# Queries of the sparse attention projected with features on the partitions, split once ahead of it, and loaded as matmul operands by DMA

## The chip, the cores and the metric

The kernel runs on one core of one Trainium2 chip. A core has five engines that run their own instruction streams in order: TensorE (PE in the profile, its weight loads PEld), VectorE (DVE), ScalarE (ACT), GpSimd (POOL) and SyncE (SP, which mostly issues DMAs). They share an on-chip memory of 128 partitions, and PE writes its products into accumulator banks of 128 partitions by 512 fp32, of which the kernel uses eight. The metric is the device time of one execution in microseconds (us), lower is better. On one core an execution is one program of 30086 recorded instructions.

## The reference

The reference is one decoder layer over 1024 positions and 1024 channels, in float32: an RMS norm and one input projection, three mixers side by side (a Mamba-2 scan, stick-breaking attention, and a sparse attention with three branches), a gated merge, an output projection, and a gated MLP with a short convolution. What matters here is the sparse attention and where its queries come from:

```python
h = rms_norm(x, pre_mix_norm[l])
proj = h @ w_in[l]                       # 512 of its columns are nsa_q: 2 groups x 4 heads x 64 features
...
sc = einsum('bqghd,bngd->bghqn', qb, kc) * scale - slopes * dist_c      # 64 compressed keys per group
p_cmp = masked_softmax(sc, dist_c >= 0)
o_cmp = einsum('bghqn,bngd->bqghd', p_cmp, vc)
... p_cmp summed over the 4 heads ranks 16 blocks of 64 keys; the best 8 are kept ...
ss = einsum('bqghd,bgqnkd->bghqnk', qb, ks) * scale - slopes * dist_s   # selected blocks
sw = einsum('bqghd,bkgd->bghqk', qb, kwb) * scale - slopes * dist_w     # window of 512
out = gate0 * o_cmp + gate1 * o_sel + gate2 * o_win
```

The query is used three times: against the compressed keys, against the selected blocks and against the window.

## The kernel before

**Products in three parts.** A float32 value is kept as a pair of rounded halves, `hi` and `lo` (type fp32r), and a product a*b is summed from a_hi*b_hi, a_hi*b_lo and a_lo*b_hi. So whatever enters such a product is first split: ScalarE copies it to fp32r (`hi`), and VectorE or GpSimd subtracts (`lo`). All of PE's instructions go through one helper, so they carry line 234; the tile names tell them apart (`ps_s`, `ps_t`, `ps_o`, `ps_b` and `dense` are accumulator banks; there are two each of `ps_s`, `ps_t` and `dense`, one each of `ps_o` and `ps_b`).

**The program's stages, in order.** (1) The start, to about 56 us: x comes in twice, by rows (for the norm's sums of squares, `square`) and by columns, and the query projection runs while the norm's factors are still being formed. `h_hi` and `h_lo` hold the columns, 8 chunks `k` of 128 channels by 1024 positions, in two halves `h` of 512 positions. The first half is first split without the norm's factor (`first_split`), so that its queries are scaled afterwards, and then normed and split again (`norm`, `high`, `low`). (2) A gate unit, and the Mamba projections (`ssm_units`), to about 310 us. (3) The sparse attention (`nsa_stage`): projections of keys and values, the compressed keys and values (two units, `unit_steps(U_CMP + s)`), the keys turned onto the partitions, then the loop over 16 tiles, from 395 to about 725 us. (4) Stick-breaking attention, the scan, the merge and the MLP, which the change does not touch.

**Queries, up to now.** `four_tiles` (L497) computes for a chunk `ci` (one of the two key groups, 256 query features) and a half `h` four tiles of 128 positions. In `tm_products` (L424) the positions are the stationary operand and the 256 features of the weights move through the array, so a result has positions on the partitions; each of the two chunks and two halves takes 8 k by 4 tiles by 3 matmuls of 256 columns. `q_out` (L528) scales a tile, for the first half by the norm's factor of its positions (`rq`, a value per partition), and `q_store` (L534) writes it to memory as `q_d[group, tile]`. The order of this stage is pinned by hand on every engine (`pin`), with two hooks at given places of the second group of products: `first_rows` and `second_rows` let PE transpose the norm's factors into a row per half (`rows`), which VectorE multiplies into x.

**The loop of the sparse attention.** Three generators are advanced in slots: `compressed` (L1024), which runs ahead and makes a tile's compressed branch, its ranking and its query operands; `maxima` (L1109), which bounds the scores; and `attend` (L1148), which makes scores and values, block by block. PE's order is the order of this program (`E.in_order[0] = True`). A slot in which there is no block takes matmuls of the gate units as filling (`fill.take`, `NSA_FILL`), two groups of three; a slot with a block takes one group where `compressed` and `maxima` have nothing to do. `NSA_SLOTS`, `NSA_START` and the lags set the slots. On the other engines and on SP's queue a scheduler places instructions.

**What a tile does with its query.** `compressed` loads the tile as it lies in memory (`q_in`, L1026), and a second time with every head twice side by side (`qd`, two DMAs, L1029). PE transposes `q_in` in two pieces, ScalarE copies them to `qT` (L1034), and PE multiplies `qT` with the compressed keys `KC`. Four lags and the softmax later PE transposes `qd` in four pieces into `p1`; ScalarE rounds all 128 rows to `Q2` (L1093) and the upper 64 to `Q1` (L1094), and VectorE leaves `Q2`'s lower half as the rest (L1099). `Q1` holds the hi part with mask rows and slopes below it, from a ring of 4 tiles; the two slope rows come by a DMA on ScalarE's queue (L1096) once per ring tile and group. `score` (L1152) multiplies `Q1` and `Q2` with the keys.

## Time and profile before

| | us |
|---|---|
| three runs, median (lowest to highest) | 2168.35 (2167.76 to 2170.72) |
| the profiled execution: its own time | 2170.24 |
| the profiled execution: span of the instructions | 2168.5 |
| PE busy in the span | 2110.4 (97%) |
| VectorE, ScalarE, GpSimd busy | 1349.0, 1209.9, 1188.1 (62%, 56%, 55%) |
| DMA, mean rate over the span | 108 GB/s |

The span is that of the profiled execution, whose own time is 1.7 us longer. In the profile's rows a start and a duration are given in us from the span's start. A matmul's duration reaches from its entry into the array to its modelled end, while the next one has already entered; what a matmul takes of PE's time is the distance from its start to the next one's start. "x4" in a row joins four instructions; an fp32 matmul that is not fp32r stands as two. In brackets stands the idle time before an instruction and what ended it. In the table by windows the columns are each engine's busy time with its count, then PE's granted clock (1.00 is full), the DMA engines' busy share and the rate.

### The profile page before, as it was taken

The page shows a single profiled execution, that of the slowest core. Times are in us where ns is not written, and L with a number is a line of the kernel's source. Part 1 is how long each engine was busy: PE and PEld are TensorE (multiplying, and loading weights), DVE is VectorE, ACT ScalarE, POOL GpSimd, SP SyncE. Part 2 cuts the span into 40 slices and gives each one's busy share as a digit, 9 for nine tenths or more (in the row PEclk, how much of TensorE's full clock was granted, in tenths as well). Part 3 has the DMA queues.
Part 4 walks back from the last instruction along what each step waited for, and adds up shares of the span by engine and source line. Part 5 has one row for each costly group of instructions (what it writes and reads, how often), then busy time and mean ns, then how long its engine had stood idle before and what let it go on. Part 6 is the DMA issues. An engine that isn't in the chain of part 4 may idle for free.

```text
span 2168.5 us, 30086 instructions
## 1 busy us (share of the span) xinstructions
PE 2110.4 (97%) x10437; PEld 1712.7 (79%) x10437; DVE 1349.0 (62%) x2665; ACT 1209.9 (56%) x2290; POOL 1188.1 (55%) x1035
## 2 busy tenths in 40 slices
PE   9999999999999999999999999999999999999997
PEld 9787888876676688888877778887778888888886
DVE  7865545247667416566547876238776677686776
ACT  6544442367867746677775553236554454476634
POOL 0276742136846834334326686557777777766733
PEclk9999999999999999999999999999999999999999
DMA  7223341321221011222344522435222223265432
GB/s 268 96 101 112 112 138 54 92 92 42 62 71 38 23 63 40 69 68 97 119 172 169 176 93 93 146 100 187 88 83 90 96 100 114 97 198 178 149 119 105
DMA packets 127457, 233.48 MB, mean 108 GB/s; under 512 B 29844, under 2 KB 43828, under 8 KB 127304
## 3 DMA queue, kind: packets, MB, share of 16 engines
q1 hardware_dynamic: 124584, 228.94, 32.0%
q10 hardware_dynamic: 2720, 2.62, 0.4%
q8 instruction: 82, 1.34, 0.3%
q14 instruction: 71, 0.58, 0.1%
HBM read 170.06 MB, written 61.45 MB: 107 GB/s over the span
## 4 chain that ended last, share of the span: by engine, by line
PE 66%; DVE 7%; ACT 3%; issue 2%; POOL 2%; DMA 1%; SPq 0%; DVEq 0%; ACTq 0%; POOLq 0%
PE dense L234 46%; PE ps_s L234 7%; PE ps_o L234 5%; PE ps_t L234 3%; PE psn L234 3%; PE ps_b L234 2%; POOL wlo L307 1%; ACT wT L1159 1%; DVE u L344 0%; DVE ps_t L1127 0%; DMA lo<-m_d 0%; DVE x L1855 0%; DVE x L2053 0%; ACT ps_b L1049 0%; ACT oT L1183 0%
## 5 line engine op out<-in xcount | busy, mean ns | idle before, releaser
L307 POOL TENSOR_TENSOR wlo<-wraw,whi 128x256 fp32r<-128x256 f32 x300 | 237.4, 823 | 236.2 <-ACT whi L302 232.5
L234 PE MATMUL dense<-h_hi,whi 128*128 128x512 f32 x656 | 262.2, 400 | 1.1 <-DVE kk L913 1.1
L234 PE MATMUL dense<-h_hi,wlo 128*128 128x512 f32 x656 | 257.6, 393 | 0.0
L234 PE MATMUL dense<-h_lo,whi 128*128 128x512 f32 x656 | 257.1, 392 | 0.0
L1170 POOL TENSOR_TENSOR wT_lo<-wT,wT_hi 128x512 fp32r<-128x512 f32 x132 | 168.2, 1289 | 66.4 <-ACT wT_hi L1169 54.6
L234 PE MATMUL dense<-x,uhi 128*128 128x512 f32 x600 | 191.4, 391 | 0.8 <-ACT x L751 0.8
L234 PE MATMUL dense<-hi,wlo 128*128 128x512 f32 x448 | 176.4, 395 | 0.3 <-POOL wlo L668 0.3
L234 PE MATMUL dense<-lo,whi 128*128 128x512 f32 x448 | 174.8, 391 | 1.1 <-POOL lo L1874 1.1
L234 PE MATMUL dense<-hi,whi 128*128 128x512 f32 x448 | 174.8, 390 | 0.0
L668 POOL TENSOR_TENSOR wlo<-wraw,whi 128x1024 fp32r<-128x1024 f32 x35 | 84.6, 2419 | 110.0 <-ACT whi L667 109.8
L234 PEld LDWEIGHTS dense<-h_hi,wlo 128*128 128x128 f32 x656 | 123.6, 188 | 27.0
L234 PEld LDWEIGHTS dense<-h_hi,whi 128*128 128x128 f32 x656 | 123.9, 189 | 24.1 <-issue 1.3
L677 POOL TENSOR_TENSOR ulo<-uf,uhi 128x1024 fp32r<-128x1024 f32 x35 | 84.2, 2405 | 106.5 <-ACT uhi L676 106.4
L234 PEld LDWEIGHTS dense<-h_lo,whi 128*128 128x128 f32 x656 | 124.0, 189 | 23.0
L302 ACT ACTIVATE whi<-wraw 128x1024 fp32r<-128x1024 f32 x76 | 80.4, 1057 | 108.4 <-PE dense L234 91.9
L234 PEld LDWEIGHTS dense<-x,uhi 128*128 128x128 f32 x600 | 112.5, 188 | 25.9 <-ACT x L751 1.7
L1393 POOL TENSOR_TENSOR s_lo<-sa,s_hi 128x512 fp32r<-128x512 f32 (+2 forms) x48 | 54.2, 1130 | 129.3 <-ACT s_hi L1392 129.3
L344 DVE SCALAR_TENSOR_TENSOR u<-dense,pv,u 128x510 f32<-128x510 f32 (+1 forms) x140 | 103.5, 742 | 34.5 <-ACT u L340 34.0
L680 POOL TENSOR_TENSOR ulo<-uf,uhi 128x1024 fp32r<-128x1024 f32 x35 | 84.1, 2402 | 41.1 <-ACT uhi L679 35.1
L234 PE MATMUL dense<-x,ulo 128*128 128x512 f32 x264 | 103.2, 391 | 0.0
L1159 ACT ACTIVATE wT<-ps_s 128x512 f32<-128x512 f32 x132 | 78.2, 595 | 39.6 <-PE ps_s L234 33.2
L234 PEld LDWEIGHTS dense<-hi,wlo 128*128 128x128 f32 x448 | 84.1, 188 | 20.3 <-issue 1.9
(591 smaller groups left out, 6132.1 us busy)
## 6 DMA issues: line engine op xcount, KB each, us to landing
wraw<-in_wfm SPq DMA_DIRECT2D x62, 512.0 KB, 3.7
wraw<-in_wup SPq DMA_DIRECT2D x48, 512.0 KB, 3.5
lo<-m_d SPq DMA_DIRECT2D x58, 256.0 KB, 3.7
g_d<-gate_e SPq DMA_DIRECT2D x48, 256.0 KB, 2.2
s_d<-o SPq DMA_DIRECT2D x48, 256.0 KB, 2.1
m_d<-u SPq DMA_DIRECT2D x44, 256.0 KB, 2.0
row<-g_d SPq DMA_DIRECT2D x36, 256.0 KB, 4.0
row<-s_d SPq DMA_DIRECT2D x32, 256.0 KB, 5.4
```

The costliest lines, as they stand in the source:

```text
L234: return pin(f(*a, **k), in_order)
L302: act(hi, raw, AF.Copy)
L307: eng.tensor_tensor(lo[:, s], raw[:, s], fl(hi[:, s]), op=OP.subtract)
L344: V.scalar_tensor_tensor(o[:, d:], ps[:, :512 - d], taps[d], o[:, d:], op0=OP.mult, op1=OP.add)
L668: eng.tensor_tensor(wlo, raws[0], fl(whi), op=OP.subtract)
L677: eng.tensor_tensor(l24, f24, fl(h24), op=OP.subtract)
L680: eng.tensor_tensor(l31, f31, fl(h31), op=OP.subtract)
L1159: act(w.rearrange("p h q -> p (h q)"), pz, AF.Exp)
L1170: P.tensor_tensor(lo, wf, fl(hi), op=OP.subtract)
L1393: (P if SB_SLO else V).tensor_tensor(s_lo[:, c0:], a[:, c0:], fl(s_hi[:, c0:]), op=OP.subtract)
```

## The change

The queries are projected the other way round: the weights are the stationary operand and 512 positions move, so a result has 128 features on the partitions and a half of the positions along them. `q_units` replaces `four_tiles`: per chunk and half 2 units by 8 k by 3 matmuls of 512 columns. All eight results are scaled by 1/8 on ScalarE as they leave; the first half's norm factor is now a row along the positions, so VectorE copies the transposed row of the first half to on-chip memory (`row0`) and GpSimd multiplies four results of 128x512 with it ahead of their store. `q_d` becomes a table of 512 features by 1024 positions. The hooks move from (3, 0) and (7, 0) of four tiles per k to (4, 0) and (7, 1) of two units per k.

At the start of the sparse attention the whole table is read back in eight pieces of 128x512, split by ScalarE and GpSimd, and written out as two tables, `qh_d` and `ql_d`: eight loads and sixteen stores on SP's queue. A tile of the loop then loads `qT` from `q_d` and the operands from these tables: the hi part to `Q1`'s upper half and to `Q2`'s upper half, the lo part to `Q2`'s lower half, 64 features by 4 heads by 128 positions in each DMA, runs of 512 bytes. The six transposes of a tile, the copies L1034, L1093 and L1094 and the subtraction L1099 are gone. The slope rows are loaded by SP. The ring of `Q1` and that of `Q2` have 5 tiles instead of 4, that of `qT` 3 instead of 1. `compressed` has one step fewer in all, with five waiting steps (`CMP_LAG`) instead of four ahead of the transposes of the softmax.

```diff
 
 T_AT = 3
+Q_ROWS = 4
+CMP_LAG = 5
 
...
 
 
-    q_d = scratch("q_d", [2, 8, 128, 256])
+    q_d = scratch("q_d", [512, T])
 
...
             pin(V.scalar_tensor_tensor(h_lo[:, k, hs(0)], x, pre[:, k:k + 1], fl(hi), op0=OP.mult, op1=OP.subtract))
 
-    def four_tiles(ci, ws, h, banks, hooks={}):
+    def q_units(ci, ws, h, banks, hooks={}):
 
         pss = [f() for f in banks]
         for k in range(8):
+            hi, lo = ws[k // 2]
             for n, ps in enumerate(pss):
                 if (k, n) in hooks:
                     hooks[k, n]()
-                tm_products(ps, ci, ws, 4 * h + n, k)
+                s = slice((k % 2) * 256 + n * 128, (k % 2) * 256 + (n + 1) * 128)
+                for m, (a, b) in enumerate(((hi, h_hi), (lo, h_hi), (hi, h_lo))):
+                    mm(ps, a[:, s], b[:, k, hs(h)], start=k == 0 and m == 0, stop=k == 7 and m == 2)
         return pss
...
     def factor(h, between=()):
 
-        rt, rq, v = [n1p.tile([128, 4], F32, name=f"r{n}", bufs=2) for n in "tqv"]
+        rt, v = [n1p.tile([128, 4], F32, name=f"r{n}", bufs=2) for n in "tv"]
         rsqrt_mean(rt, v, stats[h], DM)
...
         rb = n1p.tile([128, 4, 128], F32, name="rb")
         pin(act(rb, rt[:, :, None].to_broadcast([128, 4, 128]), AF.Copy))
-        if h == 0:
-            pin(V.tensor_scalar(rq, rt, 0.125, None, op0=OP.mult))
-        return rq, rb
+        return rb
 
...
         return r
 
-    def q_out(q, n, ps, scale, eng=None):
-        if eng is V:
-            pin(V.tensor_scalar(q[:, n], ps[:, :256], scale, None, op0=OP.mult))
-        else:
-            pin(act(q[:, n], ps[:, :256], AF.Copy, scale=scale))
+    def q_out(q, n, ps):
+        pin(act(q[:, n], ps, AF.Copy, scale=0.125))
 
     def q_store(ci, h, q):
-        pin(nc.scalar.dma_start(q_d[ci, 4 * h:4 * h + 4].rearrange("t p c -> p t c"), q))
+        pin(nc.scalar.dma_start(q_d[ci * 256:(ci + 1) * 256, hs(h)].rearrange("(n p) t -> p n t", p=128), q))
 
     def q_tile(name):
-        return wx0.tile([128, DM], F32, name=name).rearrange("p (t c) -> p t c", t=4)
+        return wx0.tile([128, DM], F32, name=name).rearrange("p (n t) -> p n t", n=2)
 
...
         for t in (6, 7):
             square(t)
-        late.append(factor(1)[1])
+        late.append(factor(1))
         norm(0, 4)
+        row0 = ev.tile([128, 512], F32, name="o")
+        pin(V.tensor_copy(row0, rows[0]))
+        rows.append(row0)
 
     def second_rows():
-        rows.append(factor_rows(late[0], ps_s))
+        rows.insert(1, factor_rows(late[0], ps_s))
 
...
     for p in range(2):
         chunk_weights(1, p)
-    pss = four_tiles(0, tm0, 0, (ps_s, ps_s, ps_t, ps_t))
+    first = q_units(0, tm0, 0, (ps_t, ps_t))
     for t in range(4):
         square(t)
-    rq, rb = factor(0, [partial(chunk_weights, 1, 2)])
-    qs = [q_tile("ulo")]
-    for n, ps in enumerate(pss):
-        q_out(qs[0], n, ps, rq[:, n:n + 1], V)
+    rb = factor(0, [partial(chunk_weights, 1, 2)])
     for t in (4, 5):
         square(t)
-    pss = four_tiles(1, tm1, 0, (ps_o, ps_d, ps_d, ps_b), {(3, 0): first_rows, (7, 0): second_rows})
-    qs.append(q_tile("uhi"))
+    second = q_units(1, tm1, 0, (ps_d, ps_d), {(Q_ROWS, 0): first_rows, (7, 1): second_rows})
+    qs = [q_tile("ulo"), q_tile("uhi")]
+    for n, ps in enumerate(first):
+        q_out(qs[0], n, ps)
     for k in range(8):
...
         if k > 1:
             low(1, k - 2)
-        for n in ((0, 3), (1,), (2,))[k] if k < 3 else ():
-            q_out(qs[1], n, pss[n], rq[:, n:n + 1])
         if k > 2:
             high(0, k - 3)
+    for n, ps in enumerate(second):
+        q_out(qs[1], n, ps)
     for h in range(2):
+        for n in range(2):
+            pin(P.tensor_tensor(qs[h][:, n], qs[h][:, n], rows[2], op=OP.mult))
         q_store(h, 0, qs[h])
...
     for k in range(8):
         low(0, k)
-    pss = four_tiles(0, tm0, 1, (ps_t, ps_t, ps_o, ps_b))
+    pss = q_units(0, tm0, 1, (ps_o, ps_b))
     qs.append(q_tile("ulo"))
     for n, ps in enumerate(pss):
-        q_out(qs[2], n, ps, 0.125)
+        q_out(qs[2], n, ps)
     q_store(0, 1, qs[2])
     all_in_order[0] = False
-    pss = four_tiles(1, tm1, 1, (ps_d, ps_s, ps_s, ps_t))
+    pss = q_units(1, tm1, 1, (ps_t, ps_t))
     qs.append(q_tile("uhi"))
     for n, ps in enumerate(pss):
-        q_out(qs[3], n, ps, 0.125)
+        q_out(qs[3], n, ps)
     q_store(1, 1, qs[3])
...
     nc.sync.dma_start(pos.rearrange("p s b l q -> p (s b l q)"), A["pos"])
     half = [slice(0, 64), slice(64, 128)]
+    qh_d, ql_d = [E.dram.tile([512, T], F32, name=n, tag=n) for n in ("qh_d", "ql_d")]
+    for g, h, n in itertools.product(range(2), range(2), range(2)):
+        r, c = slice((2 * g + n) * 128, (2 * g + n + 1) * 128), E.hs(h)
+        x, hi, lo = [ck.tile([128, 512], dt, name=f"q{m}", bufs=2) for m, dt in zip("xhl", (F32, R32, R32))]
+        nc.sync.dma_start(x, q_d[r, c])
+        act(hi, x, AF.Copy)
+        P.tensor_tensor(lo, x, fl(hi), op=OP.subtract)
+        nc.sync.dma_start(qh_d[r, c], fl(hi))
+        nc.sync.dma_start(ql_d[r, c], fl(lo))
     for s in range(2):
...
     for x in MMs + augs:
         V.memset(x, 0.0)
-    Q1s = [wk.tile([128, 512], R32, name=f"Q1_{n}", bufs=1) for n in range(4)]
+    Q1s = [wk.tile([128, 512], R32, name=f"Q1_{n}", bufs=1) for n in range(5)]
     for x in Q1s:
...
 
     def compressed(g, i):
-        qs = wk.tile([128, 256], F32, name="q_in", bufs=3)
-        nc.sync.dma_start(qs, q_d[g, i])
-        qd = wk.tile([128, 4, 2, 64], F32, name="qd", bufs=2)
-        for n in range(2):
-            nc.sync.dma_start(qd[:, :, n, :], q_d[g, i].rearrange("p (h d) -> p h d", h=4))
-        pq = ps_b()
-        for a in range(2):
-            tr(pq[:, a * 128:(a + 1) * 128], qs[:, a * 128:(a + 1) * 128], ident)
-        qT = wk.tile([128, 2, 128], F32, name="qT", bufs=1)
-        act(qT.rearrange("p a b -> p (a b)"), pq[:, :256], AF.Copy)
-        yield
-        ps = pq[:, 256:]
+        qT = wk.tile([128, 2, 128], F32, name="qT", bufs=3)
+        ts = slice(i * 128, (i + 1) * 128)
+        nc.sync.dma_start(qT, q_d[g * 256:(g + 1) * 256, ts].rearrange("(a p) t -> p a t", p=128))
+        Q1 = Q1s[(8 * g + i) % 5]
+        Q2 = wk.tile([128, 512], R32, name="Q2", bufs=5)
+        hi, lo = [x[g * 256:(g + 1) * 256, ts].rearrange("(h d) t -> d h t", d=64) for x in (qh_d, ql_d)]
+        for dst, x in ((Q1[0:64], hi), (Q2[0:64], hi), (Q2[64:128], lo)):
+            nc.sync.dma_start(fl(dst).rearrange("p (h t) -> p h t", h=4), x)
+        if i < 5:
+            nc.sync.dma_start(fl(Q1[80:82, :]), qa_d[:, g, :])
+        if g and i < 4:
+            act(Q1[64:80, :], fl(Q1[64:80, :]), AF.Copy, scale=0.0)
+        ps = ps_b()[:, :256]
         for a in range(2):
...
             V.tensor_tensor(left, left, im, op=OP.is_equal)
             V.tensor_scalar(aug[:, 64:80], left, NEG, None, op0=OP.mult)
-        for _ in range(4):
+        for _ in range(CMP_LAG):
             yield
...
         yield
 
-        Q1 = Q1s[i % 4]
-        Q2 = wk.tile([128, 512], R32, name="Q2", bufs=4)
-        p1 = ps_b()
-        for h in range(4):
-            tr(p1[:, h * 128:(h + 1) * 128], qd[:, h].rearrange("p a d -> p (a d)"), ident)
-        act(Q2, p1, AF.Copy)
-        act(Q1[0:64, :], p1[0:64], AF.Copy)
-        if i < 4:
-            nc.scalar.dma_start(fl(Q1[80:82, :]), qa_d[:, g, :])
-            if g:
-                act(Q1[64:80, :], fl(Q1[64:80, :]), AF.Copy, scale=0.0)
-        V.tensor_tensor(Q2[64:128, :], p1[64:128], fl(Q2[64:128, :]), op=OP.subtract)
-        yield
         yield
```

**Where instructions move.** PE at the start of the loop of tiles: `thi` and `h_lo` are the last value projection's operands, `q_in` the query as loaded, `KC` the compressed keys, `dense` a gate unit. Before:

```order
L234 MATMUL ps_s<-thi,h_lo 128x296
L234 MATMUL ps_b<-ident,q_in 128x128 x2
L234 MATMUL dense<-h_hi,whi 128x512
L234 MATMUL dense<-h_lo,whi 128x512
L234 MATMUL dense<-h_hi,wlo 128x512
L234 MATMUL dense<-h_hi,whi 128x512
L234 MATMUL dense<-h_lo,whi 128x512
L234 MATMUL dense<-h_hi,wlo 128x512
L234 MATMUL ps_b<-KC_2783,qT 128x128 x2
```

and with the change:

```order
L236 MATMUL ps_s<-thi,h_lo 128x296
L236 MATMUL ps_b<-KC_2578,qT 128x128 x2
L236 MATMUL dense<-h_hi,whi 128x512
L236 MATMUL dense<-h_lo,whi 128x512
L236 MATMUL dense<-h_hi,wlo 128x512
L236 MATMUL dense<-h_hi,whi 128x512
```

The product with the compressed keys now stands directly behind the projections, and all of the ten groups of gate matmuls up to the softmax's transposes (`cp`) stand behind it; before two of the ten stood ahead of it.

ScalarE at the same place (`da` belongs to the scan's decays, the third row is the slope rows' DMA). Before:

```order
L278 ACTIVATE sg<-sg 128x192
L1004 ACTIVATE da<-da 128x128
L1096 DMA Q_0_3673<-qa_d 2x512
L1034 ACTIVATE qT<-ps_b 128x256
L1096 DMA Q_1_3674<-qa_d 2x512
L1096 DMA Q_2_3675<-qa_d 2x512
L1096 DMA Q_3_3676<-qa_d 2x512
L1049 ACTIVATE ps_b,m_3713<-ps_b,m_3713 128x64 x4
```

and with the change:

```order
L280 ACTIVATE sg<-sg 128x192
L1017 ACTIVATE da<-da 128x128
L1063 ACTIVATE ps_b,m_3558<-ps_b,m_3558 128x64 x4
L278 ACTIVATE gate_e<-dense 128x512
L279 ACTIVATE gate_e<-gate_e 128x512
```

The slope rows' DMAs and the copy to `qT` have left ScalarE; the exponentials of the first softmax are next. VectorE keeps its order there: the clearing of the `Q1` ring (L1022, now L1035 and five times instead of four) stands ahead of the addition of the bias to the first scores.

SP's queue with the change, from the last key store to the second tile:

```order
L987 DMA k_d_2921<-k_3225 128x1024
L1040 DMA qT<-q_d 128x2x128
L1045 DMA Q_0_3534<-qh_d 64x4x128
L1045 DMA Q_3546<-qh_d 64x4x128
L1045 DMA Q_3546<-ql_d 64x4x128
L1047 DMA Q_0_3534<-qa_d 2x512
L1054 DMA cbias<-in_c_bias 128x256
L1040 DMA qT<-q_d 128x2x128
```

Where a tile had four DMAs (`q_in`, `qd` twice, `cbias`), it has five, and a sixth in the first five tiles of a group.

## The prediction

> **What bounds the kernel now.** I read the page first, for the busy shares and the chain that ended last.
>
> ```profile
> PE 2110.4 (97%) x10437; PEld 1712.7 (79%) x10437; DVE 1349.0 (62%) x2665; ACT 1209.9 (56%) x2290; POOL 1188.1 (55%) x1035
> PE 66%; DVE 7%; ACT 3%; issue 2%; POOL 2%; DMA 1%; SPq 0%; DVEq 0%; ACTq 0%; POOLq 0%
> ```
>
> PE is busy 97% of the span and carries two thirds of the chain, so a matmul taken away is worth its distance to the next one, unless PE waits there anyway. That differs by stage, so I read the table by windows next: a stretch of dense 512-column matmuls, and the sparse attention's loop with its beginning and its densest part.
>
> ```profile
> 100.00:125.00 25.00, 25.00 (x110) 20.33 (x109) 10.23 (x15) 11.71 (x18) 15.59 (x10) 1.00 0.32 105
> 395.40:410.00 14.60, 10.93 (x42) 8.69 (x41) 6.09 (x19) 5.68 (x19) 0.00 (x0) 0.77 0.10 29
> 410.00:722.00 312.00, 296.83 (x1517) 220.64 (x1516) 195.14 (x657) 220.38 (x502) 185.94 (x212) 1.00 0.21 62
> 550.00:600.00 50.00, 48.11 (x248) 32.94 (x247) 29.78 (x92) 44.01 (x100) 41.22 (x40) 1.00 0.23 62
> ```
>
> A 512-column matmul costs 25 / 110 = 0.227 us. From 410 to 722 us PE is busy 296.83 of 312 us, 95%: the loop is PE's, though ScalarE comes near (44.01 of 50 us from 550 on). Its beginning is another matter: PE works 10.93 of 14.60 us, at a mean granted clock of 0.77.
>
> **The loop.** Each of 16 tiles loses two transposes of `q_in` and four of `qd`. Their durations (0.27 us each) overlap; what they cost is read from starts in PE's timeline, one group of each kind with its neighbours.
>
> ```profile
> 414.13 0.60 PE L234 MATMUL ps_b<-ident,qd 128*128 128x128 f32 x4
> 414.48 0.48 PE L234 MATMUL dense<-h_hi,whi 128*128 128x512 f32 x1
> 414.80 0.39 PE L234 MATMUL dense<-h_lo,whi 128*128 128x512 f32 x1
> 415.03 0.40 PE L234 MATMUL dense<-h_hi,wlo 128*128 128x512 f32 x1
> 594.85 0.38 PE L234 MATMUL ps_b<-ident,q_in 128*128 128x128 f32 x2
> 594.99 0.47 PE L234 MATMUL ps_o<-wT_hi,V_hi 128*65 128x512 f32 x1
> 595.29 0.39 PE L234 MATMUL ps_o<-wT_hi,V_lo 128*65 128x512 f32 x1
> ```
>
> Four transposes hold PE 0.35 us, and the matmul behind them takes 0.32 to the next start where its like takes 0.23: 0.44 in all. Two hold it 0.14, and the one behind them takes 0.30 instead of 0.23: 0.21. A tile loses 0.65 us, 16 tiles 10.4 us. The other engines lose work too, by the views of the tiles `Q` and `qT`, and a wait goes, by the groups of PE:
>
> ```profile
> L1093 ACT ACTIVATE Q<-ps_b x16: 577/593/605, 415.6 to 711.7; 128x512 fp32r<-128x512 f32 x16
> L1094 ACT ACTIVATE Q<-ps_b x16: 577/584/592, 416.1 to 712.2; 64x512 fp32r<-64x512 f32 x16
> L1034 ACT ACTIVATE qT<-ps_b x16: 375/383/392, 400.4 to 696.3; 128x256 f32<-128x256 f32 x16
> L234 PE MATMUL ps_b<-ident,q_in 128*128 128x128 f32 x32 | 6.3, 280 | 1.0 <-DVE Q L1105 1.0
> ```
>
> ScalarE loses 0.593 + 0.584 + 0.383 = 1.56 us a tile, 25 us in all. With the transposes goes their wait of 1.0 us for the single bank `ps_b`. Bounds: if PE's waits in the loop grow to take half of what is freed, 5.2 us stay; if ScalarE's relief also counts where it is nearly full, 1.56 - 0.65 = 0.9 us in each of the six tiles without gate filling add 5.4, and the loop gains 10.4 + 1.0 + 5.4 = 16.8. I take 9.5: the 10.4 and the 1.0, less 1.9 because matmuls that covered other engines' latencies are gone; PE's 95% speaks for the near side.
>
> What replaces the transposes comes by DMA in shapes that no row shows. The nearest, issue and landing:
>
> ```profile
> L1029 SPq DMA_DIRECT2D qd<-q_d x32: 529/546/1135, 386.5 to 672.2; - x32
> DMA to landing us min/median/max: 2.5/2.7/3.4
> ```
>
> `qd` lands in runs of 256 bytes, the new loads in runs of 512; I take 3.4 us, the slow end. Four issues of 0.55 and a landing of 3.4 make 5.6 us. They are issued at `compressed`'s first step; `maxima` wants `Q1` nine steps later, most of a tile, and a tile takes 312 / 16 = 20 us. The ring of five is free in time: tile k's loads write where tile k-5 stood, and `compressed` runs at most three tiles ahead. SP issues one DMA more a tile, 0.55 us in 20. So the loads are hidden, at nothing; wholly uncovered they would cost 16 x 5.6 = 90 us, which is why they have a rival below.
>
> **The loop's beginning,** rows of PE, VectorE and ScalarE in order of time, and the table's stretch of low clock:
>
> ```profile
> 395.43 0.38 PE L234 MATMUL ps_b<-ident,q_in 128*128 128x128 f32 x2
> 399.18 2.51 DVE L1022 TENSOR_TENSOR Q<-edges 64x512 fp32r<-64x512 f32 x4
> 399.90 0.49 ACTq L1096 DMA_DIRECT2D Q<-qa_d  x1
> 400.44 0.38 ACT L1034 ACTIVATE qT<-ps_b 128x256 f32<-128x256 f32 x1 [2.29 <-DVE Q L1022]
> 400.88 1.22 PE L234 MATMUL ps_b<-KC,qT 128*128 128x128 f32 x4 [3.67 <-ACT qT L1034]
> 402.19 0.43 DVE L1044 TENSOR_TENSOR ps_b<-ps_b,cbias 128x256 f32<-128x256 f32 x1 [0.51 <-issue]
> 405.62 0.35 DVE L1053 TENSOR_SCALAR cp<-cp,some 128x256 f32<-128x256 f32 x1
> 409.34 0.38 PE L234 MATMUL ps_b<-ident,cp 128*128 128x128 f32 x2
> 399.30:406.10 6.80, 5.22 (x14) 4.32 (x15) 4.20 (x9) 2.00 (x9) 0.00 (x0) 0.50 0.21 61
> ```
>
> The copy to `qT` stands in ScalarE's queue behind the slope rows' DMA, and that waits for VectorE to clear the first `Q1`; PE waits 3.67 us for it. The change takes both off ScalarE, so PE does the `KC` product at 395.4, when the last projection ends. But VectorE still clears five `Q1` before it adds the bias, from 399.18 at 2.51 / 4 = 0.63 each, to 402.3, and from the addition to the end of `cp` it takes 405.97 - 402.19 = 3.8 us as before: `cp` ends at 406.1. PE's 30 gate matmuls until then last 30 x 0.227 = 6.8 us and end at 402.4. So the stall does not go, it moves behind them and is 3.7 us long; `cp` is transposed at 406.1 instead of 409.34, 3.2 us earlier. After the old stall the granted clock was 0.50 for 6.8 us. If the new one brings half that, 3.4 us at half speed cost 1.7; with none nothing, with the full 6.8 us all 3.2. Between these ends I take a gain of 1.5, as the new stall is as long as the old.
>
> The Trainium skill ("TensorE: Matmul & The Clock Gate", section "What's actually happening") has PE's clock halved after a window of about 3.4 us that was idle, until a busy one has passed, with windows that run freely. The row's 6.8 us is two such windows, so the trace agrees; by the rule a stall of 3.7 us can cost one window or two, which would leave 1.5 or nothing of this term.
>
> **The splitting ahead.** Eight loads, sixteen stores, eight ScalarE copies (0.59 us, as L1093) and eight GpSimd subtractions fall between 319 and 350 us.
>
> ```profile
> 325.00:350.00 25.00, 23.88 (x158) 21.41 (x157) 15.15 (x40) 2.28 (x6) 4.72 (x7) 1.00 0.13 45
> L1170 POOL TENSOR_TENSOR wT_lo<-wT,wT_hi 128x512 fp32r<-128x512 f32 x132 | 168.2, 1289 | 66.4 <-ACT wT_hi L1169 54.6
> 324.13 2.79 POOL L307 TENSOR_TENSOR wlo<-wraw,whi 128x256 fp32r<-128x256 f32 x4 [5.57 <-ACT whi L302]
> ```
>
> ScalarE (2.28 of 25 us) and GpSimd (4.72) have room, and PE's work on the two compressing units (23.88 of 25 us) covers them; uncovered they would cost 8 x 1.29 = 10 us. Two subtractions stand ahead of `wlo` on GpSimd, 2.6 us, and 5.57 us of idle time lie there to take them. I take a loss of 0.5, with bounds of 0 and 2.
>
> **The start.** 384 matmuls of 256 columns become 192 of 512. The 7th and the 132nd of the narrow ones, and what VectorE and GpSimd do later:
>
> ```profile
> 7.97 0.28 PE L234 MATMUL ps_t<-thi,h_hi 128*128 128x256 f32 x1
> 22.76 0.28 PE L234 MATMUL ps_b<-thi,h_lo 128*128 128x256 f32 x1
> 33.35 0.39 PE L234 MATMUL ps_t<-thi,h_lo 128*128 128x256 f32 x1 [0.75 <-DVE h_lo L548]
> 70.17 1.29 DVE L742 TENSOR_TENSOR x<-x 128x512 fp32r<-128x512 f32 x2 [1.09 <-ACT x L741]
> 74.81 2.42 POOL L668 TENSOR_TENSOR wlo<-wraw,whi 128x1024 fp32r<-128x1024 f32 x1 [74.31 <-ACT whi L667]
> 75.29 4.30 DVE L742 TENSOR_TENSOR x<-x 128x512 fp32r<-128x512 f32 x4 [0.70 <-ACT x L741]
> 78.43 0.50 PE L234 MATMUL ps_o<-x,ahi 128*128 128x512 f32 x1 [1.34 <-DVE x L742]
> ```
>
> A narrow one costs 14.79 / 125 = 0.118 us, and 384 x 0.118 - 192 x 0.227 = 1.7 us. The first half's share goes into waiting for `h_lo` at 33.35, the second half's into the wait for VectorE at 78.43. Moreover GpSimd gets four products of 128x512 ahead of the store, 1.29 us each. The rows at 70 and 75 us show what a GpSimd subtraction does to VectorE: two take 1.29 us alone, four 4.30 instead of 2.6 beside it. I count 1.2 us of delay on VectorE, which its later pauses behind ScalarE (1.09 and 0.70 above) take up. Net 0, with bounds of -0.7 and +2.
>
> The Trainium skill ("GPSIMD Engine Reference", section "Key points") says that GpSimd shares its on-chip memory interfaces with VectorE and collides with VectorE instructions that read two inputs there. That speaks against the change, and the rows at 75 us agree; rival (4) is what it would do.
>
> **Sum.** -9.5 - 1.5 + 0.5 + 0 = -10.5 us against the profiled execution's 2170.24, so 2159.7; the median of the three runs is 1.9 lower, which gives 2157.8, or 2158.
>
> **Rivals.** (1) The loop has other limits: PE's freed time becomes waits for ScalarE's exponentials, and half or less of it stays. For it stand the 44.01 of 50 us; against it, that ScalarE loses more than PE. The loop gives 5.2 or less, the rest 1: 2162 to 2168. (2) ScalarE's relief counts in full: 16.8 from the loop, up to 3.2 and 0.7 from the rest: 2148 to 2153. (3) The operands come late: SP works its DMAs off in order, and one that waits for its ring place, or for the clearing of a `Q1`, holds up the operands and the gate weights behind it. It ends slower than before once a tile waits over 10.5 / 16 = 0.66 us; at twice that it is 2168 - 10.5 + 21 = 2179. Against it: the loads are issued most of a tile ahead. (4) All four GpSimd products hold VectorE up at the start, 5.2 us, and PE behind it: 2163, so it falls in with (1).
>
> **How the numbers follow.** Mine 0.52 (2153 to 2162), (1) with (4) 0.20, (2) 0.18, (3) 0.10. A measurement of this kernel can tell 0.2%, 4.3 us, from no change. Of (1) half lies above 2164, of (3) 0.03 below 2172.7: faster 0.80, same 0.13, slower 0.07. The range runs from 2149, into (2), to 2166, into (1).
>
> **What would show it.** Right: the loop's span some 10 us shorter with about the same 5% of waits; PE's first wait there moved from `KC` to `cp` and 3 to 4 us long; no waits for `Q1` or `Q2`. Wrong: PE waiting for a DMA in the loop, or for `wT`, `oT` or `mx` longer than now; a loop that begins later than 395.4.

## The result, and the profile after

| | before | changed |
|---|---|---|
| median of six runs, us (lowest to highest) | 2168.77 (2166.64 to 2170.72) | 2153.56 (2150.80 to 2156.12) |
| the profiled execution, us | 2170.24 | 2150.80 |

The ratio is 0.993, with a 95% interval of 0.9917 to 0.9943: 15.2 us faster. The two profiled executions lie 19.4 us apart, since that of the changed kernel is the fastest of its six and that of the kernel before is 1.5 us above its median.

The first lines are those of the page of the changed kernel: PE's busy time, and the chain.

```profile
PE 2095.5 (98%) x10149; PEld 1690.1 (79%) x10149; DVE 1336.2 (62%) x2646; ACT 1197.1 (56%) x2246; POOL 1204.8 (56%) x1047
PE 79%; DVE 8%; ACT 5%; DMA 2%; issue 2%; POOL 2%; SPq 0%; DVEq 0%; ACTq 0%; POOLq 0%
```

PE's share rose to 98%. Where the time went is told by instructions that both kernels have, at the ends of the stages, by PE's starts:

| up to | before | changed | the stretch changed by |
|---|---|---|---|
| the end of the start (a `dense<-h_lo,uhi` of the gate unit) | 96.27 | 94.47 | -1.8 |
| a product of the keys' projection, behind the splitting | 357.93 | 356.19 | +0.1 |
| the end of the last projection | 395.43 | 391.10 | -2.6 |
| the first `cp` transposed (the loop's beginning) | 409.34 | 401.94 | -3.1 |
| the scan's first `ps_s<-s_lo,rtab` product (the loop, its end, and gate units up to the next stage) | 816.76 | 797.24 | -12.1 |
| the end of the span | 2168.5 | 2149.1 | +0.1 |

The last two stretches of interest as the table by windows has them, first before, then changed:

```profile
395.43:409.34 13.91, 10.23 (x38) 8.06 (x37) 6.09 (x19) 5.06 (x18) 0.00 (x0) 0.75 0.10 30
409.34:816.76 407.42, 390.60 (x1955) 293.18 (x1953) 218.63 (x725) 275.28 (x612) 236.03 (x264) 1.00 0.20 58
```

```profile
391.10:401.94 10.84, 7.42 (x37) 5.93 (x35) 6.70 (x20) 4.69 (x18) 0.15 (x2) 1.00 0.31 90
401.94:797.24 395.30, 381.66 (x1861) 285.49 (x1861) 205.81 (x709) 257.90 (x564) 236.26 (x264) 0.99 0.22 65
758.45:797.24 38.79, 34.23 (x149) 27.85 (x149) 9.49 (x24) 15.33 (x42) 10.04 (x14) 0.91 0.18 54
768.90:775.72 6.82, 6.07 (x14) 4.79 (x15) 1.38 (x2) 0.60 (x1) 0.41 (x1) 0.50 0.27 82
```

From the first `cp` to `rtab` PE runs 94 matmuls fewer (the 96 transposes less the first tile's two of `q_in`, which stood ahead of it) and the stretch is 12.1 us shorter. But in its last part, behind the loop's last `yacc`, the clock was 0.50 for 6.8 us, which it was nowhere in this stretch before. PE's and ScalarE's rows in order of time show what stands ahead of that:

```profile
765.35 0.27 PE L236 MATMUL ps_b<-ident,acu 128*128 128x128 f32 x1
766.28 0.26 ACT L1296 ACTIVATE ac<-ps_b 128x128 f32<-128x128 f32 x1
768.30 0.58 ACT L1319 ACTIVATE row<-dense 128x512 fp32r<-128x512 f32 x1
769.65 0.79 PE L236 MATMUL dense<-h_hi,whi 128*128 128x512 f32 x1 [4.04 <-DVE row L1320]
```

`row` reads out an accumulator bank (`dense`) of the next stage, which PE wants to fill again. It stands in ScalarE's queue behind `ac`, which needs the transposed `acu`; PE transposes that only after a whole unit of the next stage, and then waits 4.04 us for the bank. Before, gate units still stood between, and PE had work.

The loop's beginning, PE's rows and VectorE's:

```profile
391.10 0.61 PE L236 MATMUL ps_b<-KC,qT 128*128 128x128 f32 x4
394.86 3.11 DVE L1035 TENSOR_TENSOR Q<-edges 64x512 fp32r<-64x512 f32 x5
398.03 0.43 DVE L1058 TENSOR_TENSOR ps_b<-ps_b,cbias 128x256 f32<-128x256 f32 x1
398.13 0.39 PE L236 MATMUL dense<-h_hi,wlo 128*128 128x512 f32 x1
401.44 0.35 DVE L1067 TENSOR_SCALAR cp<-cp,some 128x256 f32<-128x256 f32 x1
401.94 0.41 PE L236 MATMUL ps_b<-ident,cp 128*128 128x128 f32 x2 [3.42 <-ACT gate_e L279]
```

The stall at `KC` is gone and stands at `cp`, 3.4 us. (The row names `gate_e`, the last thing that ended before PE went on; what PE needs is `cp`, which ended at 401.8.) The bias waits for five clearings on VectorE.

The start, PE, GpSimd and VectorE; and the splitting's GpSimd subtractions by their line's view:

```profile
30.19 2.52 POOL L594 TENSOR_TENSOR ulo<-ulo,o 128x512 f32<-128x512 f32 x2 [29.68 <-DVE o L563]
30.26 2.06 DVE L542 SCALAR_TENSOR_TENSOR x<-x,pv,ps_s 128x512 f32<-128x512 f32 x3 [0.21 <-PE ps_s L236]
32.24 1.02 DVE L548 TENSOR_TENSOR h_lo<-x,h_hi 128x512 fp32r<-128x512 f32 x1
33.84 0.68 DVE L548 TENSOR_TENSOR h_lo<-x,h_hi 128x512 fp32r<-128x512 f32 x1
40.70 2.56 POOL L594 TENSOR_TENSOR uhi<-uhi,o 128x512 f32<-128x512 f32 x2 [7.99 <-ACT uhi L532]
42.67 3.56 DVE L548 TENSOR_TENSOR h_lo<-x,h_hi 128x512 fp32r<-128x512 f32 x5
31.72 0.50 PE L236 MATMUL ps_o<-h_hi,thi 128*128 128x512 f32 x1 [0.80 <-ACT h_hi L545]
33.31 0.50 PE L236 MATMUL ps_o<-h_lo,thi 128*128 128x512 f32 x1 [0.86 <-DVE h_lo L548]
77.33 0.50 PE L236 MATMUL ps_o<-x,ahi 128*128 128x512 f32 x1 [0.16 <-DVE x L746]
```

```profile
L912 POOL TENSOR_TENSOR ql<-qx,qh x8: 1266/1290/1297, 324.0 to 347.4; 128x512 fp32r<-128x512 f32 x8
```

At 33.31 PE waits for `h_lo` as it did at 33.35 before. At 77.33 it waits 0.16 us for VectorE where it waited 1.34. The eight subtractions of the splitting took 1.29 us each between 324 and 349 us, and PE's stretch around them is as long as before.

### The profile page after: what moved, and what is told of

It is laid out like the page before. It is cut to its first block, busy times and chain, and to the rows that moved or that the text cites. A ratio compares the mean times of both kernels' runs of the same rounds, so it can differ in the third digit from the quotient of the medians.

```text
span 2149.1 us, 29505 instructions
## 1 busy us (share of the span) xinstructions
PE 2095.5 (98%) x10149; PEld 1690.1 (79%) x10149; DVE 1336.2 (62%) x2646; ACT 1197.1 (56%) x2246; POOL 1204.8 (56%) x1047
## 4 chain that ended last, share of the span: by engine, by line
PE 79%; DVE 8%; ACT 5%; DMA 2%; issue 2%; POOL 2%; SPq 0%; DVEq 0%; ACTq 0%; POOLq 0%
PE dense L236 53%; PE ps_s L236 9%; PE ps_o L236 6%; PE ps_t L236 5%; PE psn L236 3%; PE ps_b L236 3%; ACT wT L1160 1%; DMA traw<-in_wtm 1%; DVE ps_t L1128 1%; ACT wT_hi L1170 0%; POOL wlo L309 0%; DVE x L1856 0%; DVE u L346 0%; ACT whi L304 0%; DVE osq L1817 0%
## 5 line engine op out<-in xcount | busy, mean ns | idle before, releaser
L1128 DVE CUSTOM_DVE_ANT_0 ps_t<-ps_t,edges 128x256 f32<-128x256 f32 (+3 forms) x160 | 82.2, 526 | 30.8 <-PE ps_t L236 30.1
```

Of the source, the lines that this page charges most:

```text
L1128: V.tensor_tensor_reduce(pm[:, :w], pm[:, :w], edges[:, 0:w] if edge else edges[:, 640 - w:], 1.0, -3e38, op0=OP.add, op1=OP.max, accum_ou ...
```

## The experiments

Times of single executions differ by where the clock falls to a half: such a window lasts 3.41 us and costs up to 1.7 us. So the loop, from the first `cp` to the first `ps_s<-s_lo,rtab`, is also given less half of its time at half clock. It comes from one profiled execution of each kernel. Each ratio is taken against runs of the kernel before that were made beside the experiment; their medians are 2168.7 (e1 to e4), 2169.2 (e5 to e8) and 2169.4 us (e9 to e12).

| | median, us | loop, us | of it at half clock | loop less half of that |
|---|---|---|---|---|
| before | 2168.8 | 407.4 | 0 | 407.4 |
| changed | 2153.6 | 395.3 | 6.8 | 391.9 |
| e1: PE's transposes back | 2162.6 | 403.3 | 6.1 | 400.2 |
| e2: ScalarE's copies back, bunched | 2158.7 | 397.8 | 6.4 | 394.6 |
| e3: six lags | 2146.4 | 389.6 | 0 | 389.6 |
| e9: six lags, PE's transposes back | 2156.0 | 399.2 | 0 | 399.2 |
| e10: six lags, ScalarE's copies back | 2160.4 | 402.2 | 10.2 | 397.1 |
| e5: all of it back | 2165.8 | 407.6 | 0 | 407.6 |
| e11: all of it back, bank not held | 2175.0 | 415.3 | 6.8 | 411.9 |
| e4: clearing and tables moved | 2143.2 | 388.8 | 0 | 388.8 |
| e6: six lags, clearing moved | 2144.4 | 389.4 | 0 | 389.4 |

### What the loop's gain is made of

**e1.** PE's transposes alone.

```diff
-        ps = ps_b()[:, :256]
+        pq = ps_b()
+        for a in range(2):
+            tr(pq[:, 256 + a * 128:256 + (a + 1) * 128], ident, ident)
+        ps = pq[:, :256]
...
         yield
+        p1 = ps_b()
+        for h in range(4):
+            tr(p1[:, h * 128:(h + 1) * 128], ident, ident)
         yield
```

> The changed kernel, with the six transposes a tile given back to PE and to nothing else: two of `ident` ahead of the KC product and four into a bank of their own where the queries used to be turned. Nobody reads them, so what the kernel computes stays the same. Theory P (the prediction's term): PE's own time is what the loop gained, 0.65 us a tile; the median goes from 2153.6 to 2164, and the loop from the first `cp` to the scan's first `rtab` product gets 10 to 11.4 us longer. Theory W (the loop's waits are what shrank, because ScalarE is relieved): PE's transposes partly fill waits for ScalarE, and the loop gets 3 to 7 us longer; the median is 2157 to 2161.

The median rose by 9.0 us to 2162.6 (ratio to before 0.9967, 0.9956 to 0.9979), the loop by 8.0 (8.3 without the half clock). That is between the two theories, which had 10 to 11.4 and 3 to 7 for the loop.

**e2.** ScalarE's copies alone, from a constant.

```diff
...
+        act(junk[:, :256], edges[:, :256], AF.Copy)
...
+        act(junk, edges[:, :512], AF.Copy)
+        act(junk[0:64], edges[0:64, :512], AF.Copy)
```

> The changed kernel, with three copies a tile given back to ScalarE and to nothing else (128x256, 128x512 and 64x512 from a constant into a tile that nobody reads; 0.38 + 0.59 + 0.59 = 1.56 us a tile, 25 us in all). What is computed stays the same. Theory P (the prediction's choice): ScalarE is not the loop's bound; its 25 us fall into its idle time, the median rises by 0 to 2 us, to 2154 to 2156. Theory W: PE's waits in the loop shrank by 9.5 us (24.6 to 15.1 us of gaps between the first `cp` and the scan's tables) because ScalarE was relieved; with the copies back 5 to 10 us of them return, and the median is 2158 to 2163. Theory S (the waits shrank because the generator of a tile has one step fewer and the filling falls elsewhere): as theory P.

The median rose by 5.2 us, but the run doesn't test what it was made for. As the copies waited for nothing, all 48 ran between 393.8 and 433.7 us, in the first two tiles, instead of three a tile. It was made anew as e10.

**e3.** A step more per tile.

```diff
-CMP_LAG = 5
+CMP_LAG = 6
```

> The changed kernel with six lags between the softmax and its transposes instead of five, so that a tile's generator has ten steps again, as before the change. Theory S (the shorter generator made the waits shrink and moved gate matmuls into the loop): PE's waits in the loop come back, the loop gets 5 to 9 us longer; less than that where gate units stay for the end again and its 4 us stall goes. Theories P and W: only the steps move, the median stays within 3 us of 2153.6.

No theory had this: the median *fell* by 7.2 us, to 2146.4 (0.9899, 0.9882 to 0.9916). The last part of the stretch, from the last `yacc` to `rtab`, before and in e3:

```profile
776.05:816.76 40.71, 40.45 (x191) 33.55 (x189) 9.23 (x24) 16.69 (x44) 9.97 (x14) 1.00 0.19 58
```

```profile
751.95:792.55 40.60, 40.34 (x191) 33.48 (x190) 9.24 (x24) 16.59 (x44) 9.98 (x14) 1.00 0.19 58
402.97:792.55 389.58, 377.88 (x1854) 283.55 (x1855) 206.78 (x709) 259.66 (x564) 235.94 (x264) 1.00 0.22 66
```

Both run 191 matmuls there, the changed kernel 149. A tile's generator has ten steps before and in e3, nine in the changed kernel, so more slots of the loop find `compressed` and `maxima` idle and take gate units: some 42 matmuls, 9.5 us, that would have covered the loop's end were used up inside it. With ten steps the 4.04 us wait and the half clock behind it are gone. e3 has as many steps as the kernel before, so it is the better comparison for the work removed: 407.4 - 389.6 = 17.8 us. It isn't quite a clean one, as the steps stand elsewhere: the product with `KC` comes a step earlier, and six steps lie between it and the transposes of `cp` where four did.

**e5.** All the removed work back, four lags and ten steps; nobody uses its results. PE's order in the loop is that of the kernel before, instruction for instruction.

```diff
-CMP_LAG = 5
+CMP_LAG = 4
...
+            tr(pq[:, 256 + a * 128:256 + (a + 1) * 128], qT[:, a], ident)
...
+        act(junk, pq[:, 256:], AF.Copy)
+        yield
...
+            tr(p1[:, h * 128:(h + 1) * 128], ident, ident)
+        act(junk2, p1, AF.Copy)
+        act(junk2[0:64], p1[0:64], AF.Copy)
+        V.tensor_tensor(junk2[64:128], p1[64:128], fl(junk2[64:128]), op=OP.subtract)
+        yield
```

> The changed kernel's start, splitting and loads, but in the loop all the work that the change removed is given back in its old places and with its old chains: two transposes into `ps_b` and ScalarE's copy of them, a step ahead of the KC product; four transposes into `ps_b`, two ScalarE copies of the bank and VectorE's subtraction from it. Nobody reads the copies; four lags, ten steps, and PE's order in the loop is that of the kernel before. What is computed stays the same. The kernel with six lags (2146.4; first `cp` to the scan's `rtab` 389.6 us) differs from it only in that work. Theory P (the transposes alone, 0.65 us a tile, and ScalarE's part hidden): the loop gets 10 to 11 us longer, 400. Theory B (the single bank `ps_b` is held by ScalarE and VectorE until they have read it, and the steps behind it in PE's order wait): about 17 us, 405 to 408, as in the kernel before (407.4), and a median of 2162 to 2165. If the operands by DMA cost something of their own, the loop is longer than before's 407.4.

407.6 us, the number of theory B, where the kernel before took 407.4. So the operands by DMA cost little of their own: nothing against the kernel before, and 1.3 us against e12 below (406.3), which also has the slope rows on SP's queue. The removed work, with the other places of the steps in e3, is worth 18.0 us. That it is the holding of the bank, as theory B says, this run can't show.

**e9.** The transposes alone on the base of e3 (edits of e1 and e3 together).

> Six lags and the six transposes a tile given back to PE alone (nobody reads them), as in the first run but on the base whose steps are those of the kernel before. Loop without them: 389.6 us from the first `cp` to the scan's `rtab`. Theory P: 0.65 us a tile, the loop takes 400. The first run's return (8 us) repeats in theory B, 398, and the 10 us that are left to 407.6 belong to the copies, the bank or both together.

399.2 us, between the two theories (400 and 398) and 9.6 more than e3; the medians too lie 9.6 apart, or 8.9 with each taken against its own runs of the kernel before. 10.4 had been worked out from the starts of the neighbours. The other 18.0 - 9.6 = 8.4 us lie between e9 and e5. They hold what hung on the transposes (ScalarE's copies, VectorE's subtraction, and the bank that these hold) and also the places of the steps, which no run separates: e9 has six steps between `KC` and `cp`, e5 four. Groups of PE that wait, in e9 and then in e5:

```profile
L236 PE MATMUL ps_o<-wT_hi,V_hi 128*65 128x512 f32 x132 | 54.1, 410 | 1.4 <-ACT oT L1190 1.1
L236 PE MATMUL ps_s<-ident,oT 65*128 65x65 f32 x128 | 13.5, 228 | 2.2 <-ACT wT L1166 2.2
L236 PE MATMUL ps_b<-ident,cp 128*128 128x128 f32 x32 | 6.1, 273 | 1.8 <-ACT gate_e L279 1.8
L236 PE MATMUL ps_b<-ident 128*128 128x128 f32 x94 | 15.7, 276 | 2.2 <-DVE yacc L1101 1.2 <-DVE Q L1112 1.0
```

```profile
L236 PE MATMUL ps_o<-wT_hi,V_hi 128*65 128x512 f32 x132 | 53.7, 407 | 2.5 <-ACT oT L1198 2.3
L236 PE MATMUL ps_s<-ident,oT 65*128 65x65 f32 x128 | 13.7, 229 | 3.7 <-ACT wT L1174 3.5
L236 PE MATMUL ps_b<-ident,cp 128*128 128x128 f32 x32 | 6.3, 277 | 3.1 <-ACT gate_e L279 1.7 <-DVE cp L1071 1.0 <-DVE cp L1073 0.3
L236 PE MATMUL ps_b<-ident,qT 128*128 128x128 f32 x30 | 6.0, 282 | 1.4 <-DVE Q L1120 0.9 <-DVE junk L1114 0.5
L236 PE MATMUL ps_b<-ident 128*128 128x128 f32 x64 | 9.7, 273 | 0.6 <-DVE yacc L1104 0.6
```

In e5 PE waits longer for ScalarE's `wT` and `oT` (1.5 and 1.1 us in these rows) and for `cp` (1.3, which may come from the four steps). These three make 3.9 of the 8.4 us. At the transposes themselves it waits about as long in both (2.2 us in e9, 1.4 + 0.6 in e5). By the table by windows PE is also busy for 391.3 us in e5 and 387.2 in e9 with the same matmuls: a matmul that starts late, but within the duration of the one ahead of it, makes the busy time longer and shows as no wait. So the 8.4 us are spread over many places, a little in each.

**e10.** ScalarE's copies alone on the base of e3, reading what the tile has just made.

```diff
...
+        act(junk, qT.rearrange("p a b -> p (a b)"), AF.Copy)
...
+        act(J(junk2), twice(y), AF.Copy)
+        act(J(junk2[0:64]), twice(y[0:64]), AF.Copy)
```

(`twice` reads the 256 columns of `yacc` two times over, `J` views the tile in the same way.)

> Six lags and ScalarE's three copies a tile given back alone; they read what the tile has just made (`qT`, and `yacc` twice over) so that they stand where the old copies stood, one set a tile, which in the second run they did not. Nobody reads them. Theory P (ScalarE's 25 us are hidden): the loop stays at 390 to 391. Theory W (PE waits for a ScalarE that is nearly full): 0.9 us in each of the six densest tiles and more, 395 to 398.

397.1 us less the half clock, 7.5 more than e3, as theory W has it; 402.2 with it. But the copies brought waits of their own into ScalarE's queue, by the waits of ScalarE in the loop:

```profile
ACT junk L1054 <- DMA qT<-q_d: 8.7, 8, 1.9
ACT junk L1105 <- DVE yacc L1100: 4.2, 4, 2.8
```

So 7.5 us is ScalarE's 25 us and these 12.9 us of waiting together, and more than the copies alone would cost. That ScalarE's delays reach PE is shown; how much the copies' own time costs isn't.

**e11.** As e5, but the copies and the subtraction read `qT` and `yacc` instead of the bank.

> All the removed work given back as in the run with 407.6 us, with PE's order the same, but ScalarE's copies and VectorE's subtraction read `qT` and `yacc` instead of the bank `ps_b`, so that nobody holds the bank and nothing waits for PE's transposes. Nobody reads the copies. Theory B (the bank's holding costs 7 us: 18.0 less the 8 of the transposes and the 2 to 3 of the copies): 399 to 402. Theory A (the parts add to more than their sum, since they meet in the same dense tiles, bank or no bank): 406 to 408.

411.9 us, longer than e5. The run has a fault of the same kind: ScalarE's copy waits for the load of `qT`, by that line's view,

```profile
  DMA qT<-q_d: 14.1, 9
```

14.1 us in 9 times. Theory B gets no support, and theory A isn't shown by it either.

### The loop's beginning and its end

**e12.** The kernel before, with one line changed.

```diff
-            nc.scalar.dma_start(fl(Q1[80:82, :]), qa_d[:, g, :])
+            nc.sync.dma_start(fl(Q1[80:82, :]), qa_d[:, g, :])
```

> The kernel before with one line changed: the slope rows' DMA is issued from SP's queue instead of ScalarE's. Theory P (the prediction's step on the loop's beginning: ScalarE's copy to `qT` waits in its queue behind that DMA, which waits for VectorE's clearing; without it PE's stall of 3.67 us at `KC` goes to the first `cp`, 3 to 4 us long, and `cp` is transposed some 3 us earlier): the stall moves from `KC` to `cp`, the first `cp` comes 11 us instead of 14 after the last projection, and the median is 2164 to 2168. Rival: the stall stays at `KC`, since ScalarE waits for something else, and the median is 2168 to 2170.

The median fell by 4.7 us to 2164.7 (0.9977, 0.9966 to 0.9988). PE's rows:

```profile
397.56 0.71 PE L234 MATMUL ps_b<-KC,qT 128*128 128x128 f32 x4 [1.26 <-ACT qT L1034]
404.74 0.41 PE L234 MATMUL ps_b<-ident,cp 128*128 128x128 f32 x2 [0.99 <-ACT gate_e L277]
```

The first `cp` comes 404.74 - 394.52 = 10.2 us after the transposes of `q_in`, at the last projection's end, where it was 13.9. The stall moves as theory P had it, but it is shorter and in two parts (1.26 and 0.99 us). That is 3.7 of the 4.7 us; the loop behind it took 406.3 us instead of 407.4.

**e4.** In the changed kernel, GpSimd clears the `Q1`, and the scan's tables (`tables`: the lines from the `dta` products to the stores of `ac_d`, until now behind the loop) stand ahead of the last slots.

```diff
-        V.tensor_tensor(x[64:128, :], edges[64:128, :512], edges[64:128, :512], op=OP.subtract)
+        P.tensor_tensor(x[64:128, :], edges[64:128, :512], edges[64:128, :512], op=OP.subtract)
...
     for n in range(-2, 17):
+        if n == 16:
+            tables()
```

> The changed kernel with two waits taken away: GpSimd clears the five `Q1` instead of VectorE, and the scan's table products with their ScalarE copies (`acu`, `ac`, `ab`) stand ahead of the loop's last nine slots instead of behind them. By the trace of the changed kernel PE waits 3.58 us for the first `cp` behind VectorE's clearing (five times 0.63 us), and 4.04 us at the loop's end for ScalarE's `row`, which stands behind `ac`, followed by 6.8 us at half the clock. Theory P (the stall at the beginning is VectorE's clearing, and the end's stall is ScalarE's order): 3.1 us of the first and 4.0 to 7.4 of the second go, the median is 2143 to 2147. Rival: both stalls are only the place where PE's lead over the other engines shows, and come back a little later; the median stays at 2151 to 2155.

2143.2 us (0.9877, 0.9862 to 0.9892), 10.4 less than the changed kernel. The rows at the beginning, and the loop:

```profile
392.59 0.61 PE L237 MATMUL ps_b<-KC,qT 128*128 128x128 f32 x4
396.25 0.41 DVE L1059 TENSOR_TENSOR ps_b<-ps_b,cbias 128x256 f32<-128x256 f32 x1
400.14 0.41 PE L237 MATMUL ps_b<-ident,cp 128*128 128x128 f32 x2
400.14:788.95 388.81, 378.59 (x1860) 283.53 (x1860) 206.01 (x709) 257.88 (x564) 236.29 (x264) 1.00 0.21 64
```

From `KC` to `cp` it is 7.6 us instead of 10.8, with no wait, and the loop is 6.5 us shorter: both stalls were what the trace said, and don't come back later. This kernel beats both.

**e6.** e3 with the clearing on GpSimd.

> Six lags, and GpSimd clears the five `Q1` instead of VectorE. By the trace of the kernel with six lags (2146.4), PE still waits 2.2 us for the first `cp`. Theory P (that wait is VectorE's clearing): it goes, and the median is 2143 to 2145; the loop's end needs nothing, since gate units are left for it. Rival: the wait comes back in the loop's first tiles, 2146.

2144.4 us, as theory P had it. The median alone doesn't tell it from e3; the trace does, as `cp` is transposed 8.6 us after `KC` instead of 10.8, with no wait, and the loop took 389.4 us as in e3. It also beats both kernels and can't be told from e4: with ten steps the end needs no help.

### The start

**e7.** The four products with the row of norm factors on VectorE.

```diff
-            pin(P.tensor_tensor(qs[h][:, n], qs[h][:, n], rows[2], op=OP.mult))
+            pin(V.tensor_tensor(qs[h][:, n], qs[h][:, n], rows[2], op=OP.mult))
```

> The changed kernel with the four products of the queries with the row of norm factors on VectorE instead of GpSimd. Theory P (GpSimd's products cost VectorE little): VectorE, busy 29.6 of 30 us from 25 to 55, gets 4 x 0.68 = 2.7 us more, and the median rises by 1 to 3 us, to 2155 to 2157. Rival C (GpSimd beside VectorE slows VectorE by as much as it works, as in the row of the kernel before where four subtractions took 4.30 instead of 2.6 us): VectorE loses 2.7 us and wins 2.6 to 5 back; the median stays at 2151 to 2154.

2156.9 us, 3.3 more, the upper end of theory P. PE's wait at the start is back, and VectorE again has more `x` left when GpSimd's subtraction begins (74.91 us); five of them take 3.09 us alone and 4.90 beside it:

```profile
66.74 3.09 DVE L746 TENSOR_TENSOR x<-x 128x512 fp32r<-128x512 f32 x5
75.38 4.90 DVE L746 TENSOR_TENSOR x<-x 128x512 fp32r<-128x512 f32 x5 [0.70 <-ACT x L745]
78.53 0.50 PE L236 MATMUL ps_o<-x,ahi 128*128 128x512 f32 x1 [1.52 <-DVE x L746]
```

### The loads

**e8.** The three loads a tile issued at the end of its steps.

```diff
-        for dst, x in ((Q1[0:64], hi), (Q2[0:64], hi), (Q2[64:128], lo)):
-            nc.sync.dma_start(fl(dst).rearrange("p (h t) -> p h t", h=4), x)
...
+        for dst, x in ((Q1[0:64], hi), (Q2[0:64], hi), (Q2[64:128], lo)):
+            nc.sync.dma_start(fl(dst).rearrange("p (h t) -> p h t", h=4), x)
```

> The changed kernel with the three loads of `Q1` and `Q2` issued eight steps later, with the last step of a tile's generator, just ahead of its turn in the bounds; everything else stays. Theory P (the loads are hidden by the eight steps between issue and first use; three issues of 0.5 and a landing of 3.4 us make 5 us): now at most two slots of 2 us cover them, PE waits 1 to 3 us a tile, the median is 2168 to 2200. Rival (the planner's lead of a whole tile covers them wherever they stand): the median stays at 2152 to 2156.

2154.4 us, no difference. The edit didn't make the loads late: the scheduler places SP's queue, and there too the loads are issued as soon as a ring place is free. In the changed kernel, by their line's view:

```profile
L1045 SPq DMA_DIRECT2D Q<-qh_d x32: 573/586/648, 382.7 to 635.7; - x32
```

The last ones go out at 635.7 us, and PE begins the bounds that need them at 679.1, over two tiles later. No group of PE in the loop waits for a DMA. How close to its use a load may come was not found out.

## Why the prediction was right

Predicted were 2158 us, 10.5 us less; measured 2153.56, 15.2 less, in the range and just inside what was given for the likeliest case. Term by term, against the profiled pair:

- **Transposes, -10.4:** nearly right. They cost 9.6 us (e9), or 8.3 with the shorter generator (e1). The starts of the neighbouring matmuls priced them well.
- **Waits in the loop, +0.9 (1.0 for the bank less 1.9 for lost cover):** the step that failed. "I take 9.5 ... PE's 95% speaks for the near side" held the other engines' relief for nothing. What hung on the transposes is worth up to 8.4 us (e5 less e9, the places of the steps included). The 1.0 us for the bank did not go either: in the changed kernel the product with `KC` waits 0.8 us for the same instruction of VectorE (L1106, before L1105). Rival (2)'s 16.8 us are near the 17.8 to 18.0 measured with ten steps; that ScalarE's relief alone is the reason, as it has it, isn't shown.
- **What the loop gave back:** not foreseen at all. The shorter generator moved 42 gate matmuls from behind the loop into it, and the end was left with a wait of 4.04 us and a half clock behind it. The loop took 395.3 where it can take 389.6 (e3): 5.7 us. So the measured -12.1 is 17.8 less 5.7, and the -9.5 came near it by luck, because two errors of opposite sign stood in it. The order of instructions would have shown the smaller count behind the last `yacc`.
- **The loop's beginning, -1.5:** the mechanism was right: PE's first wait went from `KC` to `cp` and was 3.4 us long (3.7 predicted), because VectorE clears five `Q1` (e4, e12). The 3.2 us were got in full, -3.1, as this execution had no half clock there, a case that the prediction's "one window or two" left out. Other executions had it: see below.
- **The splitting, +0.5:** it cost 0.1 or nothing.
- **The start, 0:** -1.8. The first half gave nothing, as predicted: PE gets the first `h_lo` of the next half at 33.31 where it was 33.35, and the transposes' wait for `rb` (0.80 at 23.84 before) became one for `h_hi` (0.80 at 31.72). The second half's wide matmuls gave some 0.6 us (the next unit's first product starts at 55.35 instead of 55.94), and most of the wait for VectorE at 78.43 went, which the prediction had expected to swallow that; VectorE had two `x` left when GpSimd's subtraction of 74.3 began, where it had four before. Rival (4) was wrong: the products slowed VectorE by 0.3 us at 32.24 and 0.4 to 0.5 at 42.67 (five `h_lo` in 3.56 us, 0.61 to 0.63 each elsewhere), not by 5.2, and the same four on VectorE cost 3.3 us more (e7). How much of the 1.8 us is the change is open: e12, with the start of the kernel before, ended it at 95.28 instead of 96.27, and the traces with the changed start and no half clock in it (after, e3, e4, e5, e8, e9, e11) at 94.06 to 95.00.
- **The keys' projections, 0:** -2.6, of which up to 1.7 is a half clock at 368.57 that the profiled execution before had (e12 has it too, at 367.48), and the rest shorter waits there. The change has no instruction in this stage's products; only the order around them moved.
- **Rival (1)** was wrong: the waits did not take PE's freed time. **Rival (3)** was wrong: no wait for a load, and e5 shows the operands by DMA at 0.2 to 1.3 us.

The 4.2 us between the profiled pair and the medians fit the clock: the changed kernel's six runs have mean clocks of 0.993 to 0.996, the profiled one the highest. 0.003 of 2150 us is 6.5 us of lost clock, or about four windows of 1.7; the six lie 5.3 us apart.

What stays open is how the 8.4 us divide between ScalarE's copies, VectorE's subtraction, the holding of `ps_b` and the places of the steps: e2, e10 and e11 each brought a wait or a place of their own, and no run has the steps of the kernel before without the work.

## What to carry to other kernels

When transposes go from an engine that seems to be the bound, count what hung on them too: here the copies out of the bank, the subtraction and the bank's holding were worth up to 8.4 us, almost as much as the transposes (9.6). When a loop's step count changes, look at who fills the slots and what is left behind the loop: a stall at a stage's end can eat a third of the gain, and one more idle step gave it back. A short instruction that only prepares (a clearing, a small DMA) on a busy engine's queue is worth moving by itself: one line of the old kernel was good for 4.7 us.

## What the runs showed of the hardware that was not expected

**The half clock after a stall comes or stays away.** The changed kernel waits 3.4 us for `cp` and has a full clock behind it in its profiled execution. e1, e2, e7, e8 and e11 have much the same wait there (3.2 to 4.3 us), and each has a window at half clock, from the end of the wait or up to 1.4 us behind it; so has e10 behind a wait of 2.0 us, while e3 has none behind the same. By the table by windows of e7 and of e8:

```profile
407.51:410.92 3.41, 3.41 (x10) 2.68 (x9) 0.00 (x0) 0.00 (x0) 0.00 (x0) 0.50 0.80 228
```

```profile
403.40:406.81 3.41, 3.41 (x9) 2.65 (x8) 0.00 (x0) 0.00 (x0) 0.00 (x0) 0.51 0.65 183
```

So a single profile says little about what such a stall costs: nothing in the changed kernel, up to 1.7 us in these, and in the kernel before, where PE worked at half clock from 400.88 to 406.1, 2.6. Without the stall (e4, e6) there was no window. The Trainium skill ("TensorE: Matmul & The Clock Gate", section "What's actually happening") lets the windows run freely and says that the result varies with where work falls in them; the trace agrees: the half clocks of a trace begin whole multiples of 3.413 us apart (e1: at 34.18, 402.82 and 781.70 us, 108 and 111 windows), so the windows' bounds are known through the whole run. In the changed kernel a bound at 400.26 us cuts the stall in two, and PE is busy for about half of the window on either side; in e1 the window ahead of the half clock holds most of the stall. The changed kernel's two windows, then e1's:

```profile
396.85:400.26 3.41, 1.67 (x8) 1.05 (x6) 1.97 (x4) 1.18 (x6) 0.00 (x0) 1.00 0.66 190
400.26:403.67 3.41, 1.73 (x9) 1.51 (x10) 0.96 (x3) 2.46 (x7) 0.00 (x0) 1.00 0.70 195
```

```profile
399.41:402.82 3.41, 0.89 (x4) 0.39 (x3) 1.40 (x5) 2.12 (x10) 0.00 (x0) 1.00 0.73 195
```

PE was busy for 0.89 us there, and for 0.00, 1.36, 1.11, 1.06 and 1.46 us in the like window of e2, e7, e8, e11 and e10. So the window need not be idle, other than the prediction says of it. Over all fourteen traces, away from their ends, each window at full clock with PE busy for 0.44 of it or less was followed by one at half clock (16 windows), none with more than 0.64 was, and between these it went either way.

**In these rows GpSimd slows VectorE only where both operands are tiles in the on-chip memory, not in a bank.** Beside GpSimd's products from 30.19 to 32.71, VectorE's three `x` with one operand in the bank `ps_s` took 2.06 us, 0.69 each as always; the next one, `h_lo` from two tiles, took 1.02 us instead of 0.68. The Trainium skill ("GPSIMD Engine Reference", section "Key points") names two-input instructions of this kind for the collision, and both rows agree; what it costs depends on which of VectorE's instructions happen to fall there.
